# A two-block transformer layer on one core: products of two head pairs in one run on TensorE

## The chip, the core and the metric

The kernel runs on one core of a Trainium2 chip. TensorE (PE in the profile) multiplies, with its weight loads as a second row (PEld); VectorE (DVE), ScalarE (ACT) and GpSimd (POOL) do the elementwise work, and SyncE (SP) issues most DMAs. The metric is the device time of one execution in microseconds (us), lower is better.

## The reference, cut to what matters

Two transformer blocks stand one behind the other, batch 1, 512 tokens, width 1024, all in fp32. Each has an attention with 8 heads of width 64, and the change touches only the end of it: probabilities, transposed, times values.

```python
# first block: top-k attention, softmax over the selected keys
p = jax.nn.softmax(logits, axis=-1).astype(v.dtype)
return jnp.einsum('bqhk,bqkhd->bqhd', p, vg)
...
# second block: two branches (selected blocks, window) and a compressed one, gated and summed
p = masked_softmax(s, m_sel[:, :, None])
o_sel = jnp.einsum('bghqk,bgqkd->bqghd', p.astype(dt), v_sel)
...
p = masked_softmax(s, m_win)
o_win = jnp.einsum('bghqk,bkgd->bqghd', p.astype(dt), v_win)
...
o = g[..., 0:1] * o_cmp + g[..., 1:2] * o_sel + g[..., 2:3] * o_win
```

Around it stand projections, a retention (first block), a gated linear attention (second block, "gla" in the names), and two feed-forward layers.

## The kernel before

Every large projection is made of three matmuls on operands that are split into a high and a low part of a faster type (L298 to L300, `mm3`). Small matmuls on plain fp32 operands stand between them: the profile shows each of these as two passes (two MATMUL rows for one `matmul` in the code), except the transposes (L419), which are one pass each.

Attention is done by `attend` in tiles of 128 queries (t = 0 to 3). Tile t looks at t+1 chunks of 128 keys. For each of four head pairs j it makes an item of three steps:

- `qk`: for each head a score matmul into a bank of the two `at` banks (L838 in the first block, L1227 in the second), a VectorE reduction of scores and bias (L439, a custom instruction and the read of its accumulator), ScalarE's exp (L442); then VectorE's reciprocal (L445), the gate (L447, second block) and the scaling of both heads' probabilities `pm` (L449, two instructions).
- `tp`: for each head, t+1 transposes of `pm` into one of two `tr` banks (L419), and one ScalarE copy of them to the tile `pt` (L457).
- `out`: 2(t+1) products of `pt` and the values (L463). A product fills 64 of TensorE's 128 columns: head a=0 of a pair writes partitions 0 to 63 of the bank `ps_pv`, head a=1 partitions 64 to 127.

`pipeline` runs item i's `qk`, then item i-2's `out`, then item i-1's `tp`. Over both blocks that makes 240 products (80 and 160) and as many transposes of `pm`; 8 more transposes belong to the compressed branch. In the second block a tile's items are the compressed branch (L1247, L1279), four pairs of the selected branch and four of the window.

What stands beside attention on TensorE: projections, and in the second block also gla (L1369, L1385, L1403, L1409, and transposes of `gosb`, L419). After the last tile's products ScalarE and VectorE split the bank into `qS` (L360, L361), and the output projection `wo2` (L298 on `qS`) begins. Its residual `xT` is reloaded from DRAM by eight DMAs of 256 KB (L1087), once the last gla transposes are done with the memory, and each is scaled by VectorE (L1088).

The order on each engine is set by a scheduler of the framework at build time, from the order of the code, priorities and its own model of times; every engine then works through its list strictly in that order. In the first block's attention TensorE's list follows the code. `self.deep` holds the number of buffers of `pm` and `pt`.

Of the kernel before, what the change touches and what calls it, by code (L numbers as in the profile page):

```python
# [1 line left out]

# [4 lines left out]
F32 = mybir.dt.float32  # L7
# [7 lines left out]
P = 128  # L15
S = 512
# [148 lines left out]
class Builder:  # L165
    def __init__(self, nc, tc, ins, out, cdec, dbg=None):
        self.nc, self.tc, self.ins, self.out, self.cdec, self.dbg = nc, tc, ins, out, cdec, dbg or {}
        self.tasks, self.pend, self.ready = [], [], []
        self.order = self.plan()
        self.pools = {}  # L170
        self.every = 4
        self.deep = (4, 3)


    def open(self, name, side="left"):
# [228 lines left out]
    def rope(self, x, cos, sin, half, tmp, eng):  # L404
# [9 lines left out]
        eng.tensor_tensor(t2[:, :, half:2 * half], x[:, :, 0:half], sin[:, half:2 * half].unsqueeze(1).to_broadcast(hb), op=ALU.mult)  # L414
        eng.tensor_tensor(x, t1, t2, op=ALU.add)

    def transpose(self, out, src):
        n = src.shape[0]
        self.nc.tensor.transpose(out, src, self.c("ident", 0, n)[0:n])  # L419


    def attend(self, t, pv, score, vtok, bias, first, rowscale=None):


        nc = self.nc
        n = (t + 1) * P
        items = []
        for j in range(4):
            Pm, PT, box = [], [], []

            def qk(j=j, Pm=Pm, box=box):
                sm = self.small.tile([P, 2], F32, name="sm", tag="sm", bufs=3)
                for a in range(2):
                    h = 2 * j + a
                    sc = self.ps("at")
                    score(sc, h, n)
                    lt = self.wa.tile([P, S], F32, name="lt", tag="lt", bufs=2)
                    mn = self.small.tile([P, 1], F32, name="mn", tag="mn", bufs=4)
                    nc.vector.tensor_tensor_reduce(lt[:, 0:n], sc[:, 0:n], bias, scale=1.0, scalar=3e38, op0=ALU.add,  # L439
                                                   op1=ALU.min, accum_out=mn)  # L440
                    pm = self.wa.tile([P, S], F32, name="pm", tag="pm", bufs=self.deep[0])
                    nc.scalar.activation(pm[:, 0:n], lt[:, 0:n], AF.Exp, bias=mn, scale=-1.0, accum_out=sm[:, a:a + 1])  # L442
                    Pm.append(pm)
                rs = self.small.tile([P, 2], F32, name="rs", tag="rs", bufs=3)
                nc.vector.reciprocal(rs, sm)  # L445
                if rowscale is not None:
                    nc.vector.tensor_tensor(rs, rs, rowscale(2 * j), op=ALU.mult)  # L447
                for a in range(2):
                    nc.vector.tensor_scalar(Pm[a][:, 0:n], Pm[a][:, 0:n], rs[:, a:a + 1], None, op0=ALU.mult)  # L449

            def tp(Pm=Pm, PT=PT):
                for a in range(2):
                    tr = self.ps("tr")
                    for cc in range(t + 1):
                        self.transpose(tr[:, cc * P:(cc + 1) * P], Pm[a][:, cc * P:(cc + 1) * P])
                    pt = self.wa.tile([P, S], F32, name="pt", tag="pt", bufs=self.deep[1])
                    nc.scalar.copy(pt[:, 0:n], tr[:, 0:n])  # L457
                    PT.append(pt)

            def out(j=j, PT=PT):  # L460
                for cc in range(t + 1):
                    for a in range(2):
                        nc.tensor.matmul(pv()[a * 64:a * 64 + 64, j, :], vtok(cc, 2 * j + a), PT[a][:, cc * P:(cc + 1) * P],  # L463
                                         start=first and j == 0 and cc == 0, stop=(cc == t), skip_group_check=True)

            items.append([qk, tp, out])
        return items

# [510 lines left out]
    def block2_mix(self):  # L979
        nc, tc, ins = self.nc, self.tc, self.ins  # L980
# [83 lines left out]


        self.wa = self.open("wa", "right")
        self.deep = (6, 4)
        self.add(self.nsa(qS, kS, vt, kc, vblk, gt), 3.0)
        g = self.open("gla")
        dec = []  # L1070
# [23 lines left out]
        for m in range(8):  # L1094
# [3 lines left out]
            t = po.tile([P, S], F32, name="xz", tag="xz", bufs=4)  # L1098
# [393 lines left out]
```

## Time and profile before

| what | value |
|---|---|
| median of 3 runs | 1631.33 us (1631.3 to 1631.78) |
| the profiled execution: its own time | 1631.98 us |
| the profiled execution: span from first to last instruction | 1630.0 us |
| TensorE busy | 1607.5 us, 9093 matmul rows |
| VectorE busy | 956.4 us |
| ScalarE busy | 686.7 us |
| mean granted TensorE clock | 0.998 |
| products of attention on the trace (L463) | from 168.0 to 322.4 us (first block) and from 1043.6 to 1208.1 us (second) |

The time of an execution is its span and about 2 us around it. Busy times of TensorE are the union of matmuls whose ends are modelled, so a busy TensorE may still be slower than it could be; what one matmul costs is read from the distance between starts.

### The profile page before, as it was taken

The numbers are of one execution on the slowest core, as the hardware profiler recorded it, in microseconds if no ns is written. First come the engines' busy times: TensorE is split into PE (matmuls) and PEld (weight loads), VectorE is DVE, ScalarE is ACT, GpSimd is POOL, SyncE is SP. The second block draws the span as 40 slices with busy tenths as digits, with TensorE's granted clock in tenths as the row PEclk, the third lists the DMA queues.
The fourth block names the chain that finished last, engine by engine and source line by source line (L and its number), as shares of the span: only waits on it lengthen the run. The fifth ranks groups of instructions, "written<-read, shape, count | busy, mean of one in ns | idle before, by whom it ended". The sixth has DMA issues, their size and how long they took to land.

```text
span 1630.0 us, 23899 instructions
## 1 busy us (share of the span) xinstructions
PE 1607.5 (99%) x9093; PEld 1348.5 (83%) x9093; DVE 956.4 (59%) x2209; ACT 686.7 (42%) x1456; POOL 139.4 (9%) x290
## 2 busy tenths in 40 slices
PE   7999999999999999999999999999999999999999
PEld 5999888887888978888888899877778788888887
DVE  4489755467776764443334456675665677777221
ACT  4564655643223543223223335654653444444221
POOL 0130000021110110000000025000100000000000
PEclk9999999999999999999999999999999999999999
DMA  9223221135554533332233353121012222323331
GB/s 371 66 72 91 76 69 53 59 110 202 184 182 127 171 123 116 111 128 91 86 108 113 115 157 95 52 78 40 14 64 92 91 91 93 101 90 89 109 111 53
DMA packets 49441, 173.13 MB, mean 106 GB/s; under 512 B 6048, under 2 KB 6736, under 8 KB 48304
## 3 DMA queue, kind: packets, MB, share of 16 engines
q1 hardware_dynamic: 43376, 152.22, 29.2%
q0 software_dynamic: 5952, 19.40, 3.7%
q8 instruction: 71, 1.16, 0.3%
q14 instruction: 42, 0.34, 0.1%
HBM read 166.88 MB, written 4.19 MB: 105 GB/s over the span
## 4 chain that ended last, share of the span: by engine, by line
PE 97%; DVE 1%; DMA 1%; ACT 0%; issue 0%; POOL 0%; SPq 0%; POOLq 0%; ACTq 0%
PE ps_mm L298 27%; PE ps_mm L299 27%; PE ps_mm L300 27%; PE ps_tr L419 4%; PE ps_pv L463 3%; PE ps_at L1227 1%; PE ps_at L838 1%; PE ps_at L1176 1%; PE ps_at L780 1%; PE ps_at L913 0%; DMA xs<-in_x_dram 0%; PE ps_at L1247 0%; PE ps_mm L1403 0%; PE ps_pv L532 0%; PE ps_mm L1409 0%; PE ps_tr L390 0%
## 5 line engine op out<-in xcount | busy, mean ns | idle before, releaser
L292 ACT CAST wh<-st 128x512 fp32r<-128x512 f32 (+3 forms) x508 | 283.8, 607 | 559.1 <-PE ps_mm L299 271.3
L293 DVE TENSOR_TENSOR wl<-st,wh 128x512 fp32r<-128x512 f32 (+3 forms) x508 | 325.2, 671 | 172.7 <-ACT wh L292 171.7
L298 PE MATMUL ps_mm<-hH,wh 128*128 128x512 f32 (+1 forms) x1000 | 393.4, 394 | 4.5 <-DVE us L1454 2.2
L299 PE MATMUL ps_mm<-hL,wh 128*128 128x512 f32 (+1 forms) x1000 | 389.5, 390 | 0.3 <-DVE hL L361 0.3
L300 PE MATMUL ps_mm<-hH,wl 128*128 128x512 f32 (+1 forms) x1000 | 388.6, 389 | 0.0
L298 PEld LDWEIGHTS ps_mm<-hH,wh 128*128 128x128 f32 x1000 | 188.6, 189 | 44.9 <-DVE us L1454 2.4
L300 PEld LDWEIGHTS ps_mm<-hH,wl 128*128 128x128 f32 x1000 | 188.2, 188 | 41.1
L299 PEld LDWEIGHTS ps_mm<-hL,wh 128*128 128x128 f32 x1000 | 188.6, 189 | 38.8 <-DVE hL L361 0.5
L298 PE MATMUL ps_mm<-wh,hH 128*128 128x256 f32 (+2 forms) x672 | 194.5, 292 | 0.4 <-ACT hH L544 0.4
L299 PE MATMUL ps_mm<-wl,hH 128*128 128x256 f32 (+2 forms) x672 | 190.7, 286 | 0.0
L300 PE MATMUL ps_mm<-wh,hL 128*128 128x256 f32 (+2 forms) x672 | 188.0, 285 | 2.1 <-DVE hL L546 2.1
L298 PE MATMUL ps_mm<-fH,wh 128*128 128x512 f32 x352 | 138.8, 394 | 0.0
L299 PE MATMUL ps_mm<-fL,wh 128*128 128x512 f32 x352 | 138.7, 394 | 0.0
L300 PE MATMUL ps_mm<-fH,wl 128*128 128x512 f32 x352 | 138.5, 393 | 0.0
L298 PEld LDWEIGHTS ps_mm<-wh,hH 128*128 128x128 f32 x672 | 126.1, 188 | 4.8 <-issue 2.9
L300 PEld LDWEIGHTS ps_mm<-wh,hL 128*128 128x128 f32 x672 | 125.7, 189 | 2.9 <-DVE hL L546 2.6
L299 PEld LDWEIGHTS ps_mm<-wl,hH 128*128 128x128 f32 x672 | 126.4, 189 | 0.7 <-issue 0.2
L574 DVE SCALAR_TENSOR_TENSOR ma<-ms,silu_c,ma 128x128 f32<-128x128 f32 x224 | 77.4, 350 | 5.1
L298 PEld LDWEIGHTS ps_mm<-fH,wh 128*128 128x128 f32 x352 | 66.3, 188 | 15.4
L300 PEld LDWEIGHTS ps_mm<-fH,wl 128*128 128x128 f32 x352 | 66.1, 188 | 15.6
L299 PEld LDWEIGHTS ps_mm<-fL,wh 128*128 128x128 f32 x352 | 66.2, 188 | 15.1
L442 ACT ACTIVATE pm<-lt,mn 128x128 f32<-128x128 f32 (+3 forms) x96 | 53.7, 561 | 22.4 <-DVE mn L439 22.0
(376 smaller groups left out, 2233.6 us busy)
## 6 DMA issues: line engine op xcount, KB each, us to landing
st<-in_wup_dram SPq DMA_DIRECT2D x44, 512.0 KB, 3.3
ms<-in_wada_dram POOLq DMA_DIRECT2D x64, 256.0 KB, 3.4
st<-in_wo_dram SPq DMA_DIRECT2D x24, 512.0 KB, 3.6
st<-in_wfg_dram SPq DMA_DIRECT2D x22, 512.0 KB, 3.6
st<-in_wfu_dram SPq DMA_DIRECT2D x22, 512.0 KB, 3.5
wa<-in_wada_dram SPq DMA_DIRECT2D x8, 1024.0 KB, 11.5
st<-in_wret_dram SPq DMA_DIRECT2D x16, 512.0 KB, 3.7
st<-in_wfd_dram SPq DMA_DIRECT2D x16, 448.0 KB, 3.3
```

The lines of the kernel that those rows point to most:

```text
L292: nc.scalar.copy(hi[:, x0:x1], st[:, x0:x1])
L293: (eng or nc.vector).tensor_tensor(lo[:, x0:x1], st[:, x0:x1], hi[:, x0:x1].bitcast(F32), op=ALU.subtract)
L298: mm(ps, lh, rh, start=start, stop=False)
L299: mm(ps, lh, rl, start=False, stop=False)
L300: mm(ps, ll, rh, start=False, stop=stop)
L419: self.nc.tensor.transpose(out, src, self.c("ident", 0, n)[0:n])
L442: nc.scalar.activation(pm[:, 0:n], lt[:, 0:n], AF.Exp, bias=mn, scale=-1.0, accum_out=sm[:, a:a + 1])
L463: nc.tensor.matmul(pv()[a * 64:a * 64 + 64, j, :], vtok(cc, 2 * j + a), PT[a][:, cc * P:(cc + 1) * P], start=first and j == 0 and cc == 0, ...
L574: nc.vector.scalar_tensor_tensor(acc, w[:, k, :], s, acc, op0=ALU.mult, op1=ALU.add)
L780: nc.tensor.matmul(ps[:, 0:n], qS[:, h, :], ikS[:, i, 0:n], start=(i == 0), stop=(i == 1))
L838: nc.tensor.matmul(sc[:, 0:n], qaT[rows, h // 2, ts], kaT[rows, h // 2, 0:n], start=True, stop=True)
L1176: nc.tensor.matmul(ps[m][:, 0:64], w[:, i, m * P:(m + 1) * P], tb[:, ii, :, :].rearrange("p g n -> p (g n)"), start=(ii == 0), stop=(ii == ...
```

## The change

`out` no longer issues the products of its own pair when j is even: it puts them in a queue. When j is odd it issues both pairs' products together, first those of the pair that came last, then the earlier one's. The helper `together` keeps the first of them as the head and puts the rest behind it on TensorE (`issue_after`: an ordering edge to the head, with no semaphore). The head's operand is the `pt` that ScalarE copies last, because `tp` now transposes head a=1 first, then a=0, and the products start with a=0. The transposes of a pair are put behind their first in the same way. `pt` has five buffers instead of three (first block) and four (second). The set `started` keeps the flag that clears a half of the bank. The number of instructions on every engine is the same as before.

```diff
@@ -1,3 +1,5 @@
+import contextlib
+
 import numpy as np
 
 import concourse.bass as bass
@@ -169,7 +171,7 @@
         self.order = self.plan()
         self.pools = {}
         self.every = 4
-        self.deep = (4, 3)
+        self.deep = (4, 5)
 
 
     def open(self, name, side="left"):
@@ -414,9 +416,22 @@
         eng.tensor_tensor(t2[:, :, half:2 * half], x[:, :, 0:half], sin[:, half:2 * half].unsqueeze(1).to_broadcast(hb), op=ALU.mult)
         eng.tensor_tensor(x, t1, t2, op=ALU.add)
 
+    @contextlib.contextmanager
+    def together(self):
+
+        head = []
+
+        def run(f):
+            if head:
+                with self.tc.issue_after(head[0]):
+                    f()
+            else:
+                head.append(f().ins)
+        yield run
+
     def transpose(self, out, src):
         n = src.shape[0]
-        self.nc.tensor.transpose(out, src, self.c("ident", 0, n)[0:n])
+        return self.nc.tensor.transpose(out, src, self.c("ident", 0, n)[0:n])
 
 
     def attend(self, t, pv, score, vtok, bias, first, rowscale=None):
@@ -424,7 +439,8 @@
 
         nc = self.nc
         n = (t + 1) * P
-        items = []
+        items, queue = [], []
+        started = set() if first else {0, 1}
         for j in range(4):
             Pm, PT, box = [], [], []
 
@@ -449,19 +465,29 @@
                     nc.vector.tensor_scalar(Pm[a][:, 0:n], Pm[a][:, 0:n], rs[:, a:a + 1], None, op0=ALU.mult)
 
             def tp(Pm=Pm, PT=PT):
-                for a in range(2):
-                    tr = self.ps("tr")
-                    for cc in range(t + 1):
-                        self.transpose(tr[:, cc * P:(cc + 1) * P], Pm[a][:, cc * P:(cc + 1) * P])
-                    pt = self.wa.tile([P, S], F32, name="pt", tag="pt", bufs=self.deep[1])
-                    nc.scalar.copy(pt[:, 0:n], tr[:, 0:n])
-                    PT.append(pt)
+                with self.together() as run:
+                    for a in (1, 0):
+                        tr = self.ps("tr")
+                        for cc in range(t + 1):
+                            run(lambda: self.transpose(tr[:, cc * P:(cc + 1) * P], Pm[a][:, cc * P:(cc + 1) * P]))
+                        pt = self.wa.tile([P, S], F32, name="pt", tag="pt", bufs=self.deep[1])
+                        nc.scalar.copy(pt[:, 0:n], tr[:, 0:n])
+                        PT.insert(0, pt)
 
             def out(j=j, PT=PT):
-                for cc in range(t + 1):
-                    for a in range(2):
-                        nc.tensor.matmul(pv()[a * 64:a * 64 + 64, j, :], vtok(cc, 2 * j + a), PT[a][:, cc * P:(cc + 1) * P],
-                                         start=first and j == 0 and cc == 0, stop=(cc == t), skip_group_check=True)
+                queue.insert(0, (j, PT))
+                if j % 2 == 0:
+                    return
+
+                with self.together() as run:
+                    for j_, PT_ in queue:
+                        for cc in range(t + 1):
+                            for a in range(2):
+                                run(lambda: nc.tensor.matmul(
+                                    pv()[a * 64:a * 64 + 64, j_, :], vtok(cc, 2 * j_ + a), PT_[a][:, cc * P:(cc + 1) * P],
+                                    start=a not in started, stop=(cc == t), skip_group_check=True))
+                                started.add(a)
+                queue.clear()
 
             items.append([qk, tp, out])
         return items
@@ -1064,7 +1090,7 @@
 
 
         self.wa = self.open("wa", "right")
-        self.deep = (6, 4)
+        self.deep = (6, 5)
         self.add(self.nsa(qS, kS, vt, kc, vblk, gt), 3.0)
         g = self.open("gla")
         dec = []
```

Line numbers move with the new code: L419 becomes L434, L463 becomes L486, L439 becomes L455, L445 L461, L447 L463, L449 L465, L298 to L300 become L300 to L302, L1227 L1253 and L1088 L1114. POOL's and SP's lists are the same as before. On PE 620 of 8395 places differ, on ACT 78, on DVE 130.

Counted over TensorE's whole list, the 240 products stood in 82 unbroken runs: 36 of one product, 7 of two, 13 of three, 4 of four, 11 of five, 1 of six, 6 of seven and 4 of eight. Now they stand in 29: 3 of one, 2 of three, 6 of four, 1 of seven, 5 of eight, 1 of nine, 1 of eleven, 5 of twelve and 5 of sixteen. With two products (a=0 and a=1) to a pair and an odd one counted as a pair of its own, that is 153 pairs before and 124 now; of these, 25 runs with 48 pairs stood in the first block, and 13 with 44 stand there now. A neighbour that is narrow itself (L838, L1369, L1385) stood ahead of a run 24 times and behind one 4 times (L838); now 8 and 3 times. 69 runs were followed by a transpose, 9 by a projection; now 21 and 5.

First place, TensorE in the second block, tile t=2 (pt: transposed probabilities, vt: values, hH, hL, wh, wl: a projection). Before:

```order
L463 MATMUL ps_pv<-pt,vt 64x128 x5
L419 MATMUL ps_tr<-cst,pm 128x128 x3
L298 MATMUL ps_mm<-hH,wh 128x512
L463 MATMUL ps_pv<-pt,vt 64x128
L419 MATMUL ps_tr<-cst,pm 128x128 x3
```

and now, in the same tile:

```order
L486 MATMUL ps_pv<-pt,vt 64x128 x12
L434 MATMUL ps_tr<-cst,pm 128x128 x3
L1253 MATMUL ps_at<-kS,qS 128x384 x2
L434 MATMUL ps_tr<-cst,pm 128x128 x3
L1253 MATMUL ps_at<-kS,qS 128x384 x2
```

The five and the one of a pair, with transposes and a matmul of a projection between them, have become twelve in one run, and the projection stands behind both pairs' transposes and scores.

Second place, TensorE at the end of attention, just ahead of `wo2` (gosb: the last gla transposes stand ahead of it). Before:

```order
L419 MATMUL ps_tr<-cst,pm 128x128 x4
L463 MATMUL ps_pv<-pt,vt 64x128
L419 MATMUL ps_tr<-cst,pm 128x128 x4
L463 MATMUL ps_pv<-pt,vt 64x128 x7
L419 MATMUL ps_tr<-cst,pm 128x128 x4
L463 MATMUL ps_pv<-pt,vt 64x128
L419 MATMUL ps_tr<-cst,pm 128x128 x4
L463 MATMUL ps_pv<-pt,vt 64x128 x7
L419 MATMUL ps_tr<-cst,pm 128x128 x4
L463 MATMUL ps_pv<-pt,vt 64x128 x8
```

and now (L1253 is the score matmul of the window's last heads):

```order
L486 MATMUL ps_pv<-pt,vt 64x128 x16
L1253 MATMUL ps_at<-kS,qS 128x512 x4
L434 MATMUL ps_tr<-cst,pm 128x128 x8
L1253 MATMUL ps_at<-kS,qS 128x512 x2
L434 MATMUL ps_tr<-cst,pm 128x128 x12
L486 MATMUL ps_pv<-pt,vt 64x128 x16
L434 MATMUL ps_tr<-cst,pm 128x128 x12
L486 MATMUL ps_pv<-pt,vt 64x128 x16
```

Before, transposes of four alternate with one product and with seven; now two runs of sixteen products stand behind twelve transposes each, and the last scores stand between the transposes.

Third place, VectorE at the same end (lt: scores, rs: reciprocals, pm: probabilities, xT: the reloaded residual). Before, up to the last scaling and the rest of the residual:

```order
L439 ISA lt,mn<-ps_at,cst 128x512
L439 ISA mn 128x1
L447 TENSOR_TENSOR rs<-rs,gt 128x2
L1424 SCALAR_TENSOR_TENSOR go<-ps_mm,vecs,go 128x4x128
L449 TENSOR_SCALAR pm<-pm,rs 128x512 x2
L445 RECIPROCAL rs<-sm 128x2
L1088 SCALAR_TENSOR_TENSOR xT<-xT,vecs,rbc 128x512
L447 TENSOR_TENSOR rs<-rs,gt 128x2
L1088 SCALAR_TENSOR_TENSOR xT<-xT,vecs,rbc 128x512
L449 TENSOR_SCALAR pm<-pm,rs 128x512 x2
L1088 SCALAR_TENSOR_TENSOR xT<-xT,vecs,rbc 128x512 x6
```

Now, from the first instruction on the residual, L1114:

```order
L1114 SCALAR_TENSOR_TENSOR xT<-xT,vecs,rbc 128x512
L465 TENSOR_SCALAR pm<-pm,rs 128x512 x2
L1114 SCALAR_TENSOR_TENSOR xT<-xT,vecs,rbc 128x512
L461 RECIPROCAL rs<-sm 128x2
L1114 SCALAR_TENSOR_TENSOR xT<-xT,vecs,rbc 128x512
L455 ISA lt,mn<-ps_at,cst 128x512
L455 ISA mn 128x1
L1114 SCALAR_TENSOR_TENSOR xT<-xT,vecs,rbc 128x512
L455 ISA lt,mn<-ps_at,cst 128x512
L455 ISA mn 128x1
L463 TENSOR_TENSOR rs<-rs,gt 128x2
L1114 SCALAR_TENSOR_TENSOR xT<-xT,vecs,rbc 128x512 x3
```

and right behind it, up to the last scaling:

```order
L461 RECIPROCAL rs<-sm 128x2
L455 ISA lt,mn<-ps_at,cst 128x512
L455 ISA mn 128x1
L1114 SCALAR_TENSOR_TENSOR xT<-xT,vecs,rbc 128x512
L465 TENSOR_SCALAR pm<-pm,rs 128x512 x2
L463 TENSOR_TENSOR rs<-rs,gt 128x2
L461 RECIPROCAL rs<-sm 128x2
L465 TENSOR_SCALAR pm<-pm,rs 128x512 x2
L463 TENSOR_TENSOR rs<-rs,gt 128x2
L465 TENSOR_SCALAR pm<-pm,rs 128x512 x2
```

Before, two of the eight instructions on `xT` stood ahead of the last scaling of `pm` and six behind it; now all eight stand ahead of it, and seven of them ahead of the last three scalings.

## Rows read from the trace of the kernel before

**Rows 1.** The page: TensorE's busy time, and the chain that ended last, by engine.
```profile
PE 1607.5 (99%) x9093; PEld 1348.5 (83%) x9093; DVE 956.4 (59%) x2209; ACT 686.7 (42%) x1456; POOL 139.4 (9%) x290
...
PE 97%; DVE 1%; DMA 1%; ACT 0%; issue 0%; POOL 0%; SPq 0%; POOLq 0%; ACTq 0%
```

**Rows 2.** Windows at the end of attention: busy us (instructions) by engine, PEclk, DMA share.
```profile
1165.00:1200.00 35.00, 35.00 (x287) 25.41 (x287) 23.88 (x72) 19.98 (x49) 8.42 (x10) 1.00 0.00 1
1200.00:1212.00 12.00, 10.48 (x84) 7.47 (x82) 10.76 (x20) 6.40 (x14) 0.00 (x0) 1.00 0.54 176
```

**Rows 3.** TensorE's waits from 1043 to 1212 us: total, times, longest, in us.
```profile
PE ps_mm L298 <- ACT qS L360: 0.7, 1, 0.7
PE ps_tr L419 <- DVE pm L449: 0.5, 1, 0.5
PE ps_pv L463 <- ACT pt L457: 0.4, 1, 0.4
```

**Rows 4.** Timeline of TensorE: start us, duration, passes (xcount); two rows of a product.
```profile
307.41 1.09 PE L463 MATMUL ps_pv<-pt,va 128*64 128x128 f32 x16
308.43 0.99 PE L419 MATMUL ps_tr<-cst,pm 128*128 128x128 f32 x7
...
1067.01 0.39 PE L300 MATMUL ps_mm<-hH,wl 128*128 128x512 f32 x1
1067.24 0.40 PE L298 MATMUL ps_mm<-hH,wh 128*128 128x512 f32 x1
1067.56 0.44 PE L463 MATMUL ps_pv<-pt,vt 128*64 128x128 f32 x4
1067.93 0.50 PE L299 MATMUL ps_mm<-hL,wh 128*128 128x512 f32 x1
1068.27 0.28 PE L1227 MATMUL ps_at<-kS,qS 128*128 128x256 f32 x1
...
1196.92 0.43 PE L463 MATMUL ps_pv<-pt,vt 128*64 128x128 f32 x2
1197.28 0.66 PE L419 MATMUL ps_tr<-cst,pm 128*128 128x128 f32 x4
```

**Rows 5.** Timeline of TensorE: score matmuls ahead of a projection, and ahead of a product.
```profile
153.46 0.49 PE L838 MATMUL ps_at<-kaT,qaT 64*128 64x128 f32 x4
153.88 0.38 PE L298 MATMUL ps_mm<-wh,hH 128*128 128x256 f32 x1
...
167.60 0.49 PE L838 MATMUL ps_at<-kaT,qaT 64*128 64x128 f32 x4
168.02 0.43 PE L463 MATMUL ps_pv<-pt,va 128*64 128x128 f32 x2
```

**Rows 6.** Timeline of VectorE at the end of attention.
```profile
1199.25 0.67 DVE L439 CUSTOM_DVE_ANT_0 lt<-ps_at,cst 128x512 f32<-128x512 f32 x1
...
1201.36 0.16 DVE L445 RECIPROCAL rs<-sm 128x2 f32<-128x2 f32 x1
1202.09 0.75 DVE L1088 SCALAR_TENSOR_TENSOR xT<-xT,vecs,rbc 128x512 f32<-128x512 f32 x1 [0.56 <-DMA xT<-xd]
1202.76 0.15 DVE L447 TENSOR_TENSOR rs<-rs,gt 128x2 f32<-128x2 f32 x1
...
1203.67 0.88 DVE L449 TENSOR_SCALAR pm<-pm,rs 128x512 f32<-128x512 f32 x2
...
1205.75 3.54 DVE L1088 SCALAR_TENSOR_TENSOR xT<-xT,vecs,rbc 128x512 f32<-128x512 f32 x5 [0.54 <-DMA xT<-xd]
```

**Rows 7.** The reloads of the residual, all eight: from issue to landing.
```profile
DMA to landing us min/median/max: 2.7/5.1/5.9
```

**Rows 8.** Windows around two stops of TensorE, columns as in rows 2.
```profile
570.00:573.00 3.00, 0.68 (x4) 0.52 (x4) 1.92 (x7) 1.32 (x4) 0.00 (x0) 1.00 0.00 0
...
1272.00:1274.00 2.00, 0.50 (x4) 0.26 (x2) 1.27 (x3) 1.62 (x3) 0.00 (x0) 1.00 0.01 4
...
1275.00:1277.00 2.00, 2.00 (x7) 1.55 (x6) 1.71 (x4) 1.98 (x3) 0.00 (x0) 0.58 0.81 262
```

## The prediction

> **What bounds the kernel now.** I read the page first: TensorE is busy for 1607.5 of 1630.0 us and owns 97% of the chain that ended last, while VectorE has 59% and ScalarE 42% [rows 1]. So whatever shortens TensorE's list shortens the kernel, as long as the other engines keep up. A busy TensorE is no proof that each of its instructions is as short as it can be, so I read next, in its timeline, the distance between starts around the products, L463 [rows 4]. Three distances are to be seen there. From a run of two products (four passes) to what follows it are 0.37 us (1067.56 to 1067.93). From a run of eight (16 passes) to what follows are 1.02 us (307.41 to 308.43). From a run of one are 0.36 us (1196.92 to 1197.28), as much as from a run of two. A lone product therefore leaves half of the time empty that a pair would fill: the two heads of a pair go through the two halves of the columns side by side.
>
> Then I read TensorE's waits in the second block's attention: 1.6 us in 169, three waits, all at the very end [rows 3]. Last come the windows at that end: from 1165 to 1200 us VectorE is busy for 23.88 of 35 us, and from 1200 to 1212 us for 10.76 of 12 [rows 2]. Attention has room on VectorE nearly everywhere, but none in its last ten microseconds.
>
> **What the longer runs save.** Three terms come from rows 4 and one from rows 5.
>
> A pair costs (1.02 - 0.37) / 3 = 0.217 us. What is left of a run of one pair is 0.37 - 0.217 = 0.15 us. The step into a run costs more too: the projection ahead of it takes 0.32 us (1067.24 to 1067.56), where the one ahead of that takes 0.23. A run thus has a fixed price of 0.15 + 0.09 = 0.24 us. There are 53 fewer runs (82 to 29): 53 x 0.24 = 12.7 us saved. There are 29 fewer pairs (153 to 124): 29 x 0.217 = 6.3 us saved.
>
> The step behind a run is long as well: 0.34 us (1067.93 to 1068.27) where 0.23 is usual, so 0.11 more. Four fewer runs have a projection behind them, 0.4 us. For a transpose behind a run no row shows this price alone; it lies between nothing and those 0.11. I take the middle, 0.05, because a transpose is itself short (0.11 us, from 0.99 for seven and 0.66 for four): 48 fewer such places, 2.4 us, with bounds of 0 and 5.3.
>
> Against that, a run that stands beside another narrow matmul shares its price. Two score products take 0.42 us up to a projection (153.46 to 153.88) and also 0.42 us up to a product (167.60 to 168.02), so the product's own entry of 0.09 is not paid there [rows 5]. Such places fall from 28 to 11: 17 x 0.09 = 1.5 us given back.
>
> Together 12.7 + 6.3 + 2.8 - 1.5 = **20.3 us** less on TensorE's list, between 17.5 and 23. About a sixth of it should lie in the first block: 12 fewer runs and 4 fewer pairs there are 2.9 + 0.9 us, less the shared prices of most of the 17 places. Grouping the transposes costs and saves nothing by itself: their number and step stay.
>
> **What the end of attention gives back.** Elsewhere the waits that the change adds are hidden: between a pair's last copy and its products stand the next pair's scores or projections, and rows 3 show no wait there today. At the end there is nothing left to hide behind, and VectorE's order has changed. All eight instructions on the reloaded residual now stand ahead of the last scaling of the probabilities, and VectorE works strictly in order. What this does can be seen on a small scale in rows 6: the reciprocal ends at 1201.52, VectorE then stands for 0.56 us until the first reload has landed, and the gate behind it runs only at 1202.76. This is the cause of the 0.5 us that TensorE waits for `pm` [rows 3].
>
> From the first residual instruction to the last scaling VectorE now has 8 residuals of 0.71 us (3.54 for five), 4 pairs of scalings of 0.88, 3 reductions of 0.67 and 6 small ones of 0.16 [rows 6]: 5.7 + 3.5 + 2.0 + 1.0 = 12.2 us. On TensorE the same stretch holds a run of sixteen (0.24 + 8 x 0.217 = 2.0), four scores of 0.23 (0.9), eight transposes of 0.11 (0.9), two scores (0.5), twelve transposes (1.3), another sixteen (2.0) and four transposes (0.4), 8.0 us [rows 4]. So TensorE waits for at least 4.2 us, most of it ahead of the twelve transposes. Behind that the last two runs of sixteen each wait for a copy of `pt`, which today costs 0.4 us once [rows 3], since no seven products stand in between any more: 0.8. VectorE has gaps of its own too, for the landing (2.7 us behind an issue at the least [rows 7]) and for ScalarE's exp, about 1.5 us by the one of 0.56 here and one more for each of the last two pairs. From 6.5 the 0.5 that is paid today comes off. I take **6 us**, with bounds of 3 (VectorE finds the residuals' time while it would wait for scores) and 9 (landings of up to 5.9 us hold it as well).
>
> [...]
>
> The sum against the profiled execution: 1631.98 - 20.3 + 6 + 1 = 1618.7. The median stands 0.65 lower than that execution, so I forecast **1618 us** for the median.
>
> [...] The rows show 1.00 from 1165 to 1212 us, a stretch full of transposes and products [rows 2], so I charge the longer runs of transposes nothing. [...]
>
> **The rivals.** Chances in brackets; 0.2%, about 3.3 us, is what a measurement of this kernel can tell from no change.
> - Forecast: the list shortens by about 20, the end gives 6 to 8 back: 1614.5 to 1622 (0.58).
> - The end costs more, and the clock falls there. Speaking for it: VectorE is at 90% in the last 12 us [rows 2]. Waits of 9 us, and the lower level over some 10 us, of which half the matmul time is lost once (5 us): -20.3 + 14 gives 1625, or 1622 to 1629 (0.18).
> - The end is cheap: VectorE's residuals fall into gaps, the waits are under 3 us and the clock stays: 1610 to 1614.5 (0.16).
> - Slower: each head waits for its copy, and everything on TensorE behind it. The joined products are 24 runs by design (two of a tile in the first block, four in the second), so a mean wait of 0.85 us at each would eat the 20.3; at 1.1 us the time is 1638. It decides from 1.0 us on. The only such wait today is 0.4 us [rows 3], and work of projections still stands ahead of most heads (0.03).
> - Nearly nothing is left, by a part of both: 1629 to 1635 (0.05).
>
> The likeliest case gives the time, 1618. The range 1613 to 1625 leaves out about one in ten at either end. Of the fifth case 0.04 lie within 0.2%; faster by more holds 0.93, slower 0.03.
>
> **What the changed profile would show.** Runs of 16 products with 2.0 us from start to next start confirm price and pairs; 2.0 us for a run of twelve would refute them. TensorE's list should be level with before up to 160 us, some 3 us ahead behind the first block's attention, and 13 ahead at the start of `wo2`. There should be one wait of about 4 us of a transpose for `pm` at the end, with residuals ahead of the scaling on VectorE, and perhaps a stretch at the lower clock behind it. The forecast fails if waits for `pt` appear ahead of heads in the middle of attention, or if the end costs more than 10 us.

## The result and the profile after

The changed kernel takes **1621.03 us** (median of four executions, 1619.51 to 1621.89), against 1631.55 us of the kernel before in the same comparison: a ratio of 0.9933, 95% interval 0.9921 to 0.9945. A later comparison with five more executions gave 1621.70 us and 0.9940 (0.9927 to 0.9954). The forecast was 1618, with 1613 to 1625. It is faster, by 10 us where 13 were forecast.

From the page of the changed kernel, with the columns of [rows 1]:

```profile
span 1619.0 us, 23849 instructions
...
PE 1591.9 (98%) x9093; PEld 1346.6 (83%) x9093; DVE 954.1 (59%) x2209; ACT 685.3 (42%) x1456; POOL 138.8 (9%) x290
```

TensorE's busy time fell by 15.6 us, the span only by 11.0. So some of the gain came back as waiting. TensorE's waits from 1043 to 1215 us (columns of [rows 3]) say where:

```profile
PE ps_tr L434 <- DVE rs L461: 4.8, 1, 4.8
PE ps_at L1253 <- DVE mn L455: 1.3, 1, 1.3
PE ps_tr L434 <- DVE pm L465: 0.9, 2, 0.6
PE ps_mm L300 <- ACT qS L362: 0.7, 1, 0.7
PE ps_pv L486 <- ACT pt L474: 0.7, 1, 0.7
PE ps_tr L434 <- ACT pt L474: 0.3, 1, 0.3
```

These are 8.7 us where [rows 3] had 1.6. TensorE's timeline at the end of attention shows them in order:

```profile
1178.26 1.97 PE L486 MATMUL ps_pv<-pt,vt 128*64 128x128 f32 x32
1180.15 1.19 PE L1253 MATMUL ps_at<-kS,qS 128*128 128x512 f32 x4
1181.71 1.06 PE L434 MATMUL ps_tr<-cst,pm 128*128 128x128 f32 x8 [0.36 <-DVE pm L465]
1184.05 0.73 PE L1253 MATMUL ps_at<-kS,qS 128*128 128x512 f32 x2 [1.28 <-DVE mn L455]
1189.60 2.88 PE L434 MATMUL ps_tr<-cst,pm 128*128 128x128 f32 x12 [4.82 <-DVE rs L461]
1192.41 1.97 PE L486 MATMUL ps_pv<-pt,vt 128*64 128x128 f32 x32
...
1199.68 0.96 PE L300 MATMUL ps_mm<-qS,wh 128*128 128x512 f32 x3 [0.68 <-ACT qS L362]
```

The run of 32 passes (sixteen products) takes 1.89 us from start to next start (1178.26 to 1180.15); 2.0 was forecast. The stop of 4.82 us stands ahead of the twelve transposes. VectorE's timeline ahead of it:

```profile
1185.18 0.16 DVE L463 TENSOR_TENSOR rs<-rs,gt 128x2 f32<-128x2 f32 x1
1185.26 2.07 DVE L1114 SCALAR_TENSOR_TENSOR xT<-xT,vecs,rbc 128x512 f32<-128x512 f32 x3
1187.24 0.16 DVE L461 RECIPROCAL rs<-sm 128x2 f32<-128x2 f32 x1
1187.32 0.67 DVE L455 CUSTOM_DVE_ANT_0 lt<-ps_at,cst 128x512 f32<-128x512 f32 x1
...
1187.91 0.75 DVE L1114 SCALAR_TENSOR_TENSOR xT<-xT,vecs,rbc 128x512 f32<-128x512 f32 x1
1188.58 0.88 DVE L465 TENSOR_SCALAR pm<-pm,rs 128x512 f32<-128x512 f32 x2
```

Between the gate of one pair (1185.18) and its scaling (1188.58) stand four residual instructions (2.82 us) and a reduction. It ends at 1189.46 (1188.58 + 0.88), and the transposes start at 1189.60. (The view puts the wait down to `rs`, the small instruction on VectorE next to that scaling, which ends at 1189.60.)

The windows around the stop, and those around 573 us in both kernels (columns of [rows 2]), first the changed kernel:

```profile
571.00:574.00 3.00, 2.13 (x8) 1.92 (x9) 2.97 (x8) 2.46 (x7) 1.30 (x2) 0.53 0.00 0
574.00:577.00 3.00, 3.00 (x16) 3.00 (x15) 3.00 (x8) 2.35 (x6) 1.03 (x2) 0.50 0.00 0
...
1185.00:1188.00 3.00, 0.00 (x0) 0.00 (x0) 3.00 (x10) 0.81 (x2) 0.00 (x0) 0.59 0.04 15
...
1186.00:1192.00 6.00, 2.40 (x11) 2.21 (x12) 5.39 (x16) 1.94 (x6) 0.00 (x0) 0.50 0.00 0
```

then the kernel before:

```profile
574.00:577.00 3.00, 2.98 (x25) 2.98 (x26) 3.00 (x6) 1.94 (x5) 1.54 (x2) 1.00 0.00 0
...
1159.00:1162.00 3.00, 3.00 (x18) 2.01 (x14) 1.82 (x7) 1.77 (x5) 0.00 (x0) 0.54 0.00 0
...
1275.00:1278.00 3.00, 3.00 (x9) 2.36 (x8) 2.71 (x5) 2.80 (x4) 0.00 (x0) 0.55 0.54 175
```

The changed kernel runs at a lower clock (0.50) around 574 us and at the end: there the clock falls within the stop, while TensorE does nothing (0.59 from 1185 to 1188 us), and is still low behind it (0.50 over 1186 to 1192 us, in which TensorE is busy for 2.40 us). The kernel before had two such stretches elsewhere, at 1159 (0.54) and at 1275 us (0.55).

I compared the start of the same place of TensorE's list in both traces (the list is equally long, so the n-th matmul row is comparable wherever the order agrees):

| place | before, us | after, us | ahead |
|---|---|---|---|
| ahead of the first products | 165.16 | 165.22 | -0.1 |
| behind the first block's attention | 328.81 | 327.60 | 1.2 |
| ahead of the second block's attention | 1037.63 | 1038.57 | -0.9 |
| ahead of the last runs, matmul 7200 | 1196.13 | 1180.49 | 15.6 |
| sixth matmul of `wo2` | 1210.51 | 1200.97 | 9.5 |
| last matmul | 1625.85 | 1614.78 | 11.1 |

So 1.2 us were won in the first block, 2.1 lost to the clock around 574 us, 16.5 won in the second block's attention, 6.1 given back at its end, and 1.5 won because the stretch at 1275 us is absent. The stretches at 574 and at 1275 us come and go between executions of one list (experiments 2 and 8), so neither the 2.1 nor the 1.5 can be put down to the change.

### The profile page after: what moved, and what is told of

It is laid out like the page before. It is cut to its first block, busy times and chain, and to the rows that moved or that the text cites. A ratio compares the mean times of both kernels' runs of the same rounds, so it can differ in the third digit from the quotient of the medians.

```text
span 1619.0 us, 23849 instructions
## 1 busy us (share of the span) xinstructions
PE 1591.9 (98%) x9093; PEld 1346.6 (83%) x9093; DVE 954.1 (59%) x2209; ACT 685.3 (42%) x1456; POOL 138.8 (9%) x290
## 4 chain that ended last, share of the span: by engine, by line
PE 96%; DVE 1%; ACT 1%; DMA 1%; issue 0%; POOL 0%; SPq 0%; POOLq 0%; ACTq 0%
PE ps_mm L300 28%; PE ps_mm L301 27%; PE ps_mm L302 27%; PE ps_tr L434 3%; PE ps_pv L486 2%; PE ps_at L864 1%; PE ps_at L1253 1%; PE ps_at L1202 1%; PE ps_at L806 1%; PE ps_at L939 0%; DMA xs<-in_x_dram 0%; PE ps_at L1273 0%; PE ps_pv L558 0%; PE ps_tr L392 0%; PE ps_tr L938 0%
## 5 line engine op out<-in xcount | busy, mean ns | idle before, releaser
L300 PE MATMUL ps_mm<-hH,wh 128*128 128x512 f32 (+1 forms) x1000 | 393.8, 394 | 4.5 <-DVE us L1480 2.2
L302 PE MATMUL ps_mm<-hH,wl 128*128 128x512 f32 (+1 forms) x1000 | 388.8, 389 | 0.0
L300 PEld LDWEIGHTS ps_mm<-hH,wh 128*128 128x128 f32 x1000 | 189.8, 190 | 44.1 <-DVE us L1480 2.4
L302 PEld LDWEIGHTS ps_mm<-hH,wl 128*128 128x128 f32 x1000 | 189.0, 189 | 40.9
L300 PE MATMUL ps_mm<-wh,hH 128*128 128x256 f32 (+2 forms) x672 | 195.2, 293 | 0.0
L302 PE MATMUL ps_mm<-wh,hL 128*128 128x256 f32 (+2 forms) x672 | 187.8, 285 | 0.2 <-DVE hL L572 0.2
L300 PE MATMUL ps_mm<-fH,wh 128*128 128x512 f32 x352 | 138.8, 394 | 0.0
L302 PE MATMUL ps_mm<-fH,wl 128*128 128x512 f32 x352 | 138.5, 393 | 0.0
L300 PEld LDWEIGHTS ps_mm<-wh,hH 128*128 128x128 f32 x672 | 126.5, 189 | 5.9 <-issue 4.0
L302 PEld LDWEIGHTS ps_mm<-wh,hL 128*128 128x128 f32 x672 | 125.6, 189 | 1.1 <-DVE hL L572 0.7
L300 PEld LDWEIGHTS ps_mm<-fH,wh 128*128 128x128 f32 x352 | 66.3, 188 | 15.4
L302 PEld LDWEIGHTS ps_mm<-fH,wl 128*128 128x128 f32 x352 | 66.1, 188 | 15.5
```

What stands on the lines that cost most here:

```text
L300: mm(ps, lh, rh, start=start, stop=False)
L302: mm(ps, ll, rh, start=False, stop=stop)
```

## The experiments

Eleven runs, in groups; those of a group stood beside the same executions of the kernel before (1631.6 to 1631.8 us). "List" is the order of instructions on one engine.

**1. Residuals behind the last scaling.** The eight instructions on `xT` are queued behind the last scaling on VectorE.

```diff
-                    nc.vector.tensor_scalar(Pm[a][:, 0:n], Pm[a][:, 0:n], rs[:, a:a + 1], None, op0=ALU.mult)
+                    self.last = nc.vector.tensor_scalar(Pm[a][:, 0:n], Pm[a][:, 0:n], rs[:, a:a + 1], None, op0=ALU.mult).ins
...
-            nc.vector.scalar_tensor_tensor(self.xT[:, m, :], self.xT[:, m, :], self.v("final", m), r1bc, op0=ALU.mult, op1=ALU.mult)
+            with self.tc.issue_after(self.last):
+                nc.vector.scalar_tensor_tensor(self.xT[:, m, :], self.xT[:, m, :], self.v("final", m), r1bc, op0=ALU.mult, op1=ALU.mult)
```

> The changed kernel, with the eight VectorE instructions on the reloaded residual queued behind the last scaling of the probabilities. Theory (they cause TensorE's stop at the end of attention, and the stop the half clock behind it): the waits of 4.8 and 1.3 us for rs and mn shrink to under 1 us together and the twelve transposes behind them take 1.3 instead of 2.8 us, so 6 to 7 us less than the changed kernel, 1614 to 1615. Rival A (the chain of scores, reduction and exp sets the end anyway): 1620.5 to 1621.5, the waits stay. Rival B (the stop moves behind the products, because the split of the last bank into qS now stands behind 6 us of residuals): a wait for qS of 3 us or more at the first matmul of the output projection, 1617 to 1620.

Measured: 1613.44 us, ratio 0.9889 (0.9876 to 0.9903). Its TensorE waits from 1043 to 1215 us:

```profile
PE ps_pv L486 <- ACT pt L474: 2.1, 2, 1.4
PE ps_mm L300 <- ACT qS L362: 0.7, 1, 0.7
PE ps_tr L434 <- DVE pm L465: 0.6, 1, 0.6
PE ps_tr L434 <- ACT pt L474: 0.2, 1, 0.2
```

and a window over the end:

```profile
1178.00:1192.00 14.00, 11.11 (x128) 9.14 (x124) 12.26 (x33) 8.29 (x20) 0.00 (x0) 1.00 0.44 146
```

The waits are 3.6 us instead of 8.7, and the clock stays at 1.00. The edit is worth 7.6 us (8.3 by the second measurement of the changed kernel): the residuals were the cause of the stop, and the stop that of the half clock. Neither rival holds: the stop is gone, and the wait for `qS` stays 0.7. With the edit the scheduler also put four of the twelve transposes behind the first run of sixteen (eight rows of TensorE's list differ), so that the last lists are not quite the same. The other traces agree on the clock: all five with a stop of 4.82 us there (the changed kernel twice, experiment 3 twice, experiment 6) show the lower clock in it or right behind it (0.50 in a window of each of the changed kernel's two, experiment 3's first and experiment 6's; in experiment 3's second the twelve transposes take 2.80 us to the next start, as against 2.81 in the changed kernel), and the first kernel of experiment 4, which keeps the residuals ahead but has waits of at most 1.8 us, stays at 1.00 from 1184 to 1195 us.

**2. The same edit on the kernel before.**

> The kernel before with the same edit alone (two of the eight residual instructions stood ahead of its last scaling, now none). Theory: only the 0.5 us that TensorE waited for pm can go, 1630.8 to 1631.5, not to be told from before. Rival (the residuals cost the kernel before as much as the changed one): 4 us or more less, below 1628.

Measured: 1631.58 us, ratio 1.0000 (0.9991 to 1.0009). The residuals cost the old order nothing that can be measured (the wait of 0.5 us for `pm` is gone from its trace); only the new order put them in the way. Its trace has one thing more, at 574 us:

```profile
571.00:574.00 3.00, 1.17 (x4) 0.88 (x5) 2.70 (x8) 2.47 (x7) 0.36 (x1) 0.83 0.00 0
574.00:577.00 3.00, 3.00 (x17) 3.00 (x18) 3.00 (x7) 1.96 (x5) 1.24 (x2) 0.60 0.00 0
```

Up to there its list is that of the kernel before, whose trace shows 1.00 at that place. So the lower clock there belongs to single executions, not to the change.

**3. Unlike heads no longer alternate.** In a first kernel a run has, for each pair, all products of a=0 and then all of a=1. In a second the loop over a stands ahead of that over the pairs too: all of a=0 of both pairs, then all of a=1. VectorE's and ScalarE's lists stay as in the changed kernel.

```diff
-                        for cc in range(t + 1):
-                            for a in range(2):
+                        for a in range(2):
+                            for cc in range(t + 1):
```

> The changed kernel with the products of a run in another order: for each head pair first all of head a=0, then all of a=1, so that the two column halves of TensorE no longer alternate. Runs, operands and number of products stay. Theory (two products side by side in the column halves cost 0.217 us, and one alone costs as much): a run of 4(t+1) products has 2(t+1) pairs now; with the halves apart it has 4(t+1)-3 steps if neighbours of unlike heads still go side by side at the three seams, 4(t+1) if not. Over 24 runs that is 54 or 120 steps more, 11.7 or 26 us: 1633 or 1647. Rival (a product's price is its two passes, wherever it stands): 1620 to 1622.

> The changed kernel with the products of a run in the order: all of head a=0 of both pairs, then all of head a=1, so that unlike heads meet once in a run instead of three times (pairs apart) or at every step (the changed kernel). In the kernel with pairs apart a run of 16 took 2.50 us, of 12 1.73, of 8 1.08, where the changed kernel has 1.90, 1.46, 1.02: at each seam the halves overlapped for some 1.2 to 1.7 products. Theory (a lone product costs the 0.217 us of a pair, and only the overlap at a seam is hidden): 14 steps for 16 products, so 3.2 us for a run of 16, 2.3 for one of 12, 1.5 for one of 8; over 24 runs some 16 us more than the changed kernel, 1634 to 1639. Rival (the loss with pairs apart came from the three seams, not from the halves): less loss than with pairs apart, 1622 to 1626.

Measured: 1626.26 us (0.9968, 0.9956 to 0.9980) for the first, 1636.60 us (1.0029, 1.0019 to 1.0040) for the second, so 5.2 and 15.6 us more than the changed kernel (4.6 and 14.9 by its second measurement). Timeline rows of a run of sixteen products, first kernel:

```profile
1174.41 2.57 PE L486 MATMUL ps_pv<-pt,vt 128*64 128x128 f32 x32
1176.91 0.66 PE L434 MATMUL ps_tr<-cst,pm 128*128 128x128 f32 x4
```

and second kernel:

```profile
1179.41 3.33 PE L486 MATMUL ps_pv<-pt,vt 128*64 128x128 f32 x32
1182.67 0.66 PE L434 MATMUL ps_tr<-cst,pm 128*128 128x128 f32 x4
```

From start to next start a run of sixteen takes 2.50 and 3.26 us, against 1.89. A product that meets none of the other half costs a whole pair here, as the prediction had it (14 steps of 0.217 and 0.15 make 3.19 of the 3.26 us). In the first kernel I was wrong about the seams: I charged 11.7 us, counting one product hidden at each. The rows give (16 x 0.217 + 0.15 - 2.50) / 0.217 = 5.2 products hidden at three seams, 1.7 each. With that the second kernel was forecast at some 16 us more, and came at 15 to 16.

**4. One pair to a run.** `out` issues its own pair's products in one run, without the queue over two pairs. It was run twice with the residuals as the change has them, and once with late residuals.

```diff
                 queue.insert(0, (j, PT))
-                if j % 2 == 0:
-                    return
```

> The changed kernel without the queue over two pairs: each pair's products stand in one run of their own, as soon as its transposes are copied. TensorE's list then has 55 runs instead of 29, and 126 pairs of products instead of 124. Theory (a run has a fixed price of 0.24 us, and a transpose behind a run 0.05): 26 x 0.29 + 2 x 0.217 = 8 us more than the changed kernel, 1627 to 1630. Rival (the gain is all in products side by side, a run has no price of its own): 0.4 us more, 1621 to 1622. In both the residual instructions still stand ahead of the last scalings, so a stop of some 4 us should remain at the end of attention.

> A second look at the kernel with runs of one pair's products. By the price of a run (0.24 us and 0.05 behind it) its list should be 8 us longer than that of the changed kernel; by its first look it is some 2.5 us longer up to 1180 us. Theory of the first look: again level with that.

> Runs of one pair's products (no queue over two pairs), with the residual instructions behind the last scaling, so that it compares with the changed kernel with late residuals (1613.4) without the stop at the end. First theory (a run of products has a price of 0.29 us wherever it stands): 26 x 0.29 + 2 x 0.217 = 8 us more, 1621 to 1622. Second theory (the price belongs to each change of kind along the list; where the products leave, unlike neighbours meet, and only 6 of the changes disappear in the second block): 2 to 3 us more, 1615.5 to 1616.5.

Measured: 1619.87 us (0.9924, 0.9912 to 0.9937), in the single execution of the second run 1617.77, and with late residuals 1616.36 (0.9902, 0.9889 to 0.9916). With the stop out of the way, then, 26 fewer runs and 2 fewer pairs are worth 1616.36 - 1613.44 = 2.9 us; by my price of a run they were worth 8. The two medians alone would not carry the 2.9: the four executions with one pair to a run go from 1613.81 to 1616.91, and their trace has a stretch at the lower clock that the other lacks (1.00 there), at a cost of 1.6 us by the places of the list:

```profile
1260.00:1263.00 3.00, 3.00 (x9) 2.32 (x8) 3.00 (x6) 2.26 (x3) 0.00 (x0) 0.50 0.29 115
```

But its waits are shorter by 1.5 us, and with waits and clock taken out (the table in the next section) TensorE's list is 3.2 us longer with one pair to a run. So 8 is excluded, and some 3 holds. The queue over two pairs brought next to nothing as the change was made: at the end it costs as much in waiting and clock as it saves on the list.

At the one place where I compared a vanished run row by row, the price is right. Timeline of the kernel with one pair to a run and late residuals, around the products of a pair in tile t=2:

```profile
1129.04 1.06 PE L1303 MATMUL ps_pv<-pt,vblk 128*128 128x128 f32 x8
1130.03 0.88 PE L483 MATMUL ps_pv<-pt,vt 128*64 128x128 f32 x12
1130.83 0.55 PE L434 MATMUL ps_tr<-cst,pm 128*128 128x128 f32 x3
1131.13 0.95 PE L1251 MATMUL ps_at<-kS,qS 128*128 128x384 f32 x4
```

and the same place with runs of two pairs and late residuals:

```profile
1128.11 1.06 PE L1306 MATMUL ps_pv<-pt,vblk 128*128 128x128 f32 x8
1129.00 0.49 PE L434 MATMUL ps_tr<-cst,pm 128*128 128x128 f32 x3
1129.25 0.95 PE L1254 MATMUL ps_at<-kS,qS 128*128 128x384 f32 x4
```

The stretch takes 2.09 us with the run of six products and 1.14 without: 0.95, of which three pairs are 0.65, so 0.30 for the run itself. But the run's neighbours change too. I counted along TensorE's timeline (from 160 to 330 and from 1043 to 1215 us) how often one row's array shape (`128*128`, `128*64`, `64*128`, `64*64`) differs from the next one's:

| kernel | runs, both blocks | shape changes, first block | second block |
|---|---|---|---|
| before | 82 | 66 | 170 |
| one pair to a run, late residuals | 55 | 64 | 119 |
| two pairs, late residuals | 29 | 56 | 91 |

From 82 to 55 runs 53 changes of shape went, about two for a run. From 55 to 29 it was 36, 1.4 for a run: where a run left, other narrow work (scores of the first block, gla) now meets wide work. So fewer changes went with each run, but 1.4 for 2 explains only a part of the missing 5 us; the rest is open.

**5. The head is the operand that is copied first.** Late residuals, two pairs in the queue, but the earlier pair's products first and a=0 transposed first.

```diff
-                queue.insert(0, (j, PT))
+                queue.append((j, PT))
-                    for a in (1, 0):
+                    for a in (0, 1):
```

> The changed kernel with late residuals, but with the queue turned round: the earlier pair's products first, transposes and operands in the order a=0, a=1, so that the head's operand is the one that is copied first instead of last. TensorE's list then has 68 runs of products (55 in the second block) with 146 pairs, against 29 with 124, since the scheduler issues the early head as soon as it is ready and puts other work between it and the rest. Theory (what counts is what stands side by side in the list): about the second block of before, 1627 to 1629.5. Rival (queueing two pairs is enough, the order in the queue is a detail): 1613 to 1615.

Measured: 1630.27 us, ratio 0.9988 (0.9979 to 0.9997). That is a little above the range that I gave, and the rival falls: with the head turned round 1.5 us are left of 18, about what the first block brings. The queue and the order of the two heads were turned in one edit, so their shares are not told apart. Timeline of this kernel in tile t=2:

```profile
1120.36 0.43 PE L486 MATMUL ps_pv<-pt,vt 128*64 128x128 f32 x2
1120.72 0.62 PE L1254 MATMUL ps_at<-kS,qS 128*128 128x384 f32 x2
1121.27 0.43 PE L486 MATMUL ps_pv<-pt,vt 128*64 128x128 f32 x2
```

Lone products stand between scores again, 0.36 us each. Here the ordering edge to the head kept the rest behind it, not beside it (68 runs instead of 29). The rest stood beside it only where all of it was ready when the head was.

**6. Scores of a pair side by side in the first block.** For t=2 and t=3 64 columns of the second head go first, then the first head, then the rest of the second.

```diff
+                    head = score(banks[1], 2 * j + 1, 64).ins
+                    with self.tc.issue_after(head):
+                        head = score(banks[0], 2 * j, n).ins
+                    with self.tc.issue_after(head):
+                        score(banks[1], 2 * j + 1, n, 64)
```

> The changed kernel with the two score matmuls of a head pair held side by side in the first block, tiles t=2 and t=3: 64 columns of the second head go first (they wait for its bank), then the first head's matmul, then the rest of the second head's. Theory (scores of one head use one half of TensorE's rows; alone they take as long as both heads side by side, 1.05 us at 512 columns and 0.84 at 384, and the change left six of these pairs apart where five were apart before): 3 x 1.05 + 3 x 0.84 = 5.7 us saved less some 0.16 for each of eight extra matmuls of 64 columns, so 4.4 us less than the changed kernel, 1616.6, all of it between 160 and 330 us. Rival (the first block's small gain has another cause, scores side by side save nothing): 1621 to 1622.5.

Measured: 1618.83 us, ratio 0.9919 (0.9905 to 0.9933), 2.2 us less than the changed kernel, or 2.9 by its second measurement. Behind the first block's attention its list is 3.9 us ahead of the changed kernel's, near the 4.4 expected. The two traced executions lie 4.4 us apart (1617.4 and 1621.76); why the medians lie only 2.2 to 2.9 apart is not shown. A pair of 384 columns in the changed kernel:

```profile
221.87 0.91 PE L864 MATMUL ps_at<-kaT,qaT 64*128 64x384 f32 x2
222.71 0.33 PE L434 MATMUL ps_tr<-cst,pm 128*128 128x128 f32 x1
222.96 0.91 PE L864 MATMUL ps_at<-kaT,qaT 64*128 64x384 f32 x2
223.80 0.33 PE L434 MATMUL ps_tr<-cst,pm 128*128 128x128 f32 x1
```

and here (the four passes begin with the first head's 384 columns):

```profile
221.47 0.43 PE L872 MATMUL ps_at<-kaT,qaT 64*128 64x64 f32 x2
221.83 0.33 PE L434 MATMUL ps_tr<-cst,pm 128*128 128x128 f32 x1
222.09 0.91 PE L872 MATMUL ps_at<-kaT,qaT 64*128 64x384 f32 x4
222.93 0.55 PE L434 MATMUL ps_tr<-cst,pm 128*128 128x128 f32 x3
```

Two lone heads take 0.84 us each; together they take 0.84. The 64 columns alone cost 0.36 (221.47 to 221.83), not the 0.16 that I had charged.

**7. Both edits.** The scores of experiment 6, and the residuals behind the splits of `qS` and gla (`last` is the last of these splits on VectorE), so further back than in experiment 1.

```diff
+        with self.tc.issue_after(self.last), self.tc.issue_after(last):
+            for m in range(8):
+                nc.vector.scalar_tensor_tensor(self.xT[:, m, :], self.xT[:, m, :], self.v("final", m), r1bc, op0=ALU.mult, op1=ALU.mult)
```

> The changed kernel with both edits: scores of a pair side by side in the first block, and the residual instructions behind the split of the last bank and of gla. If the two savings add (some 4 us of the list in the first block, 7.6 at the end): 1609 to 1611. If the first block's saving is lost later: 1612.5 to 1614, as with late residuals alone.

Measured: **1609.74 us**, ratio 0.9866 (0.9852 to 0.9879). It is 3.7 us less than experiment 1, near the 3.9 by which experiment 6 shortens the list, so the two savings add. TensorE's waits at the end are 3.9 us, as good as the 3.6 of experiment 1, so the place further back shows no gain of its own. This is the best version: 22 us less than the kernel before, twice what the change brought.

**8. The changed kernel once more**, with no edit.

> The changed kernel once more, for more executions beside the others: 1619.5 to 1622. If the stretch at half clock near 571 us belongs to single executions and not to the change, it need not be in this trace; if it belongs to the change, it is there again.

Measured: 1621.70 us (the numbers stand with the result). The half clock near 574 us is in this trace too (0.50 from 574 to 577); together with experiment 2 it is neither bound to the change nor rare. The stretch that the kernel before has at 1275 us is in this trace (0.58 from 1266 to 1269) and not in the first one of the same list. Behind the stop the lower clock lasts longer here (0.53 still from 1192 to 1195, where the first trace has 0.93).

## Why the prediction was right, and where it was off

The mechanism was right in its three parts: the list shortens, the end gives a part back by VectorE's order, and the clock takes a little more. To set each beside its term I took the time from TensorE's row 1000 (at 135 us) to its last row apart: waits are its idle times of over 0.15 us, the lower clock is taken to cost half of the busy time at 0.50, and the list is what is left. The half is an estimate: in the changed kernel a 128x256 matmul of a projection takes 0.21 us from start to start at 0.50 (574.03 to 574.24) and 0.12 at 1.00 (254.01 to 254.13). Differences from the trace of before, in us:

| trace | list | waits | lower clock | together |
|---|---|---|---|---|
| forecast | -20.3 | 6 | 1 | -13.3 |
| changed kernel | -19.1 | 6.9 | 1.1 | -11.1 |
| changed kernel, second trace | -19.1 | 7.8 | 2.8 | -8.5 |
| late residuals (experiment 1) | -19.0 | 2.1 | -1.7 | -18.6 |
| one pair to a run, late residuals | -15.8 | 0.6 | 0.0 | -15.2 |

Experiment 2, whose list is that of before, gives -0.4 for the list, so the columns are good to about that.

- **Pairs side by side**: right. The runs' lengths (1.02, 1.46 and 1.90 us for 8, 12 and 16 products where they alternate) are 0.15 + n x 0.217 for n pairs of products, and experiment 3 shows that the halves are the reason.
- **The list as a whole**: right in size, 19.1 where 20.3 were forecast with 17.5 as the lower bound. Of it 1.3 us lie in the first block and the rest in the second.
- **The price of a run**: the step "a run thus has a fixed price of 0.15 + 0.09" is mis-sized as soon as it is multiplied by the number of runs. At the one place compared it holds (0.30 with what stands behind). Summed, the first 27 runs and pairs that disappear bring 15.2 us (1631.58 to 1616.36, 27 x 0.5 were to be expected), the next 26 runs 2.9 instead of 8. That the whole comes out is partly luck: the first half is under-priced, the second over-priced. Which neighbours pay for it each time is not settled here.
- **About a sixth of the 20.3 in the first block**: this step failed. It was 1.2 us instead of 3.4. One more pair of scores stood apart (a score matmul alone takes as long as two, 1.05 us at 512 columns), which the prediction's count of the list did not look for; that is about half of what is missing, and the other half stays open. Experiment 6 takes this cost away, and that of five pairs that stood apart already.
- **The end gives back 6**: right in cause, small by one. The waits rose from 1.6 to 8.7 us, by 7.1: a stop of 4.82 where 4.2 was the least, `pt` waits of 1.0 where 0.8 was charged. The 6.1 of the table of places is another sum: the waits and the lower clock there, less some 2 us that the list still saves.
- **The clock, 1 us**: no run shows this term of the sum, which was the author's estimate. What the runs show is that the clock falls at the stop (0.50 over 1186 to 1192 us), and that it costs more than 1 us. The twelve transposes take 2.81 us to the next start (1189.60 to 1192.41) where the sum had 1.3, so 1.5 us are lost. By the reckoning of the table the end loses 1.4 us here and 2.2 to 2.9 in the four other traces with this stop. The stretch at 574 us costs 2.1 here and was in no sum; it comes and goes between executions, as does that at 1275 us. The one at 1159 us is in both traces of the old list (0.68 in experiment 2) and in neither of the changed one. In the first pair of traces these stretches outside the end nearly cancel, which is luck too.
- **The rival with the lower clock over some 10 us of the end** did not come: in the changed kernel the clock fell within a stop of 4.82 us and was back at 0.93 from 1192 to 1195, with twelve more transposes and the last run of products still to come. Nor did the transposes lower it in the window of experiment 1: 1.00 over 14 us with 32 transposes (4.3 us of TensorE's 11.1 busy ones) between products and scores, and no wait above 1.4 us. What transposes alone would do no run shows. A shorter wait than that of the stop came with a lower clock too: in the changed kernel TensorE waits for 1.99 us up to 571.87 us, and the clock is at 0.53 from 571 to 574 and at 0.50 from 574 to 577 us.
- **Heads that wait for their copies**: no such wait in the middle of attention. From 1043 to 1180 us the trace has a single wait, of 0.6 us for `pm`, and none from 150 to 330 us.

## What to carry to other kernels

Here narrow matmuls that use half of the array paid in full unless one of the other half stood beside them in the list (0.36 us for one product, 0.37 for two), and this can be read from one view: compare the distance between starts of a run of one with that of a run of two. The edge, which only queues work behind a head, kept it together where the head was what became ready last (29 runs, against 68 in experiment 5). After a reordering, look at what the scheduler put on the other engines at the end of the stretch: here eight instructions of 0.7 us on VectorE, which nobody had touched, cost 7.6 of the 18 us that were there.

## What the runs showed that was not expected

- Two products that followed those of the other half did not have to alternate one by one here: at a seam some 1.7 products were hidden (sixteen products in 2.50 us with three seams, 3.26 with one, 1.89 when they alternate).
- A score matmul of 64 columns and 64 rows, alone, takes 0.36 us, as much as a lone product [rows 4]; at 384 columns it takes 0.84.
- A change of array shape cost time on both sides here: 0.32 instead of 0.23 us for the step from a projection into products [rows 4], and 0.30 instead of 0.25 for three transposes behind them (experiment 4's rows), the 0.05 that the prediction had put between its bounds. What makes these steps longer the rows do not show.
- The lower clock around 574 us appeared in the trace of one kernel and not in that of another with the same list up to there (from 574 to 577 us 0.60 in experiment 2, 1.00 in the kernel before), at a cost of 1.1 us by the places of the list (2.1 in the changed kernel). Differences of this size between two single traces of this program say nothing about a change.
